# A hand-planned trunk kernel: the rank of weight preparation, and two constants of a matmul's estimate, in the planner that fixes the order of issue

## The chip, the cores and the metric

One Trainium2 chip, one of its cores. The metric is device time in microseconds (us) from launch to end; lower is better. TensorE (PE) multiplies, VectorE (DVE), ScalarE (ACT) and GpSimd (POOL) do elementwise work, and SyncE (SP) issues the loads.

## The reference

Two decoder layers on 256 tokens of width 1024, then a final RMSNorm, all in float32.

```
for layer in range(2):
    h = rms_norm(x, mix_norm[layer])
    x = x + (gdn_shortconv_mixer if layer == 0 else nsa_mixer)(h, ...)
    x = x + square(relu(rms_norm(x, mlp_norm[layer]) @ w_up)) @ w_down
return rms_norm(x, final_norm)

gdn_shortconv_mixer(h):                       # the first mixer
    qkv, z, a, b, b_gate, c_gate, hs = split(h @ w_in)
    q, k, v = silu(causal_conv4(qkv))         # 8 heads x 64
    g = -exp(a_log) * softplus(a + dt_bias);  beta = sigmoid(b)
    o = gated_delta_rule_chunked(l2norm(q), l2norm(k), v, g, beta)
    y_a = rms_norm(o) * silu(z);  y_b = b_gate * causal_conv3(c_gate * hs)
    return concat(y_a, y_b) @ w_out
```

The delta rule inverts a unit lower-triangular matrix for each head and each of two halves of the sequence (c = 0 and 1 here), and passes a state from the first half to the second. The second mixer is sparse attention with three branches.

## The kernel before

**Arithmetic.** A float32 weight is split in two fp32r halves: `uh` (ScalarE copies it to fp32r) and `ul` (VectorE subtracts `uh` from the weight in its staging tile `st`). Activations `x` are split likewise, and each product is three matmuls of 128x128 by 256 columns: `hi*xh`, `hi*xl`, `lo*xh` (`mm256`).

**Weights.** 105 MB stream through four staging tiles `st` (two units of 128x1024 each). A unit of weights is prepared by `splits(0)` or `splits(1)` (odd and even units): one ScalarE and one VectorE instruction. There are four buffers for prepared units (UB = 4); a unit's buffer is free again, and the next split may begin, when TensorE has read the unit (flag `ud`). An emptied staging tile lets SP issue its next load.

**Streams and planner.** All engines issue strictly in the order that the program was written in, and that order comes from `Order`, which plays the kernel through with estimated durations when it is built. The work is a set of generators, "streams". Each asks for an engine, a PSUM bank, a flag or a token. `run` picks the stream that could start earliest by the estimates; of several with the same start it picks the lower rank `prio`, then the older stream (index `i`). An engine with a queue of ready streams gives all of them the same start, so there the rank decides. The streams are: the loads (rank 0), the two `splits` (rank `SPLIT`), `main` (rank `MAIN` = 9, or -1 when its clock account `debt` is over a limit), which issues all projections and the matmuls of the MLPs in order, and whatever these spawn. A spawned stream without a rank of its own gets one here:

```
    def spawn(self, gen, prio=None):
        c = self.cur
        if prio is None:
            prio = 1 if c is None or c.prio in (MAIN, SPLIT) else c.prio
```

and an engine counts as free a little before its instruction ends (`OVER`: 80 ns on VectorE), while the next instruction of the same stream can start only at that end.

**The first mixer.** `main` issues the projections K (`proj_ko`, 8 units of 512 columns), z/a/b (`proj_tok`, 8 units of 528, twelve matmuls of 264 columns each), V, Q, C, H, B (`proj_m`, four units of 24 matmuls each) and the output projection (`proj_out`, 8 units; its units 0 to 3 read `yb` of the short convolution, 4 to 7 read `ya` of the delta rule). Beside it runs the chain (rank `CHAIN` = 0): the convolution of K (`conv_evac`: `pre`, a multiplication and three multiply-adds on `cvconv`, a tanh, a product into `K`; two `pre` buffers), `zab`, `betas`, `decay`, the norms of K (`chain_k`), and `chain_main` (solutions, state). Spawned from these, without a rank of their own: `spans` and its `products` (the decay masks `E`; `gt` on POOL or VectorE), `chain_q`, `invert(c)` (`keys`: `wide` on ScalarE, transposes on TensorE, `KB` on VectorE; `scores`: `al`; then `lc`, `tt`, `uc`, and for five levels matmuls of 32x32 with `ys`, `tt`, `uc` between), `diagonal` and `output` (`o`, `osq`, `oss`, `ya`). The convolutions of V, the evacuations of Q, C, H, B (`prepool`, `CG`, `bgt`), and `values` (`bv`) are spawned by `main`. Convolutions of Q and H run on POOL (`cvpool`, `CG`, `tap`). `Norm.finish` (the sum over squares, `ncol`, `rbc`) has rank 0 in all five norms.

**Estimates.** `Timed.cost` gives the planner a duration for each instruction; for a matmul it goes by the columns m of the weights and n of the moving operand. These estimates don't change what an instruction does.

Of the kernel before, what the change touches and what calls it, by code (L numbers as in the profile page):

```python
# [11 lines left out]
F32R = mybir.dt.float32r  # L12
# [20 lines left out]
PK, PW, PR, F1, GZ, ZP, LD, RT, P2 = 1, 0, 1, 1, 1, 1, 1, 21, 8  # L33
KPOOL, VPOOL, CVB = (), (), {'conv': 4, 'pool': 2}
CHAIN, TOK_FIRST = 0, False
TICK, BUSY = 10240 / 3, 1500.0
MAIN, SPLIT, SHARE, LIMIT, FLOOR, CAP, SPARE = 9, 0, 0.5, 300, -1500.0, 4000.0, 1
ORDER1 = ('kk', 'q0', 'kc', 'vg', 'cmp', 'q1', 'wo')


# [116 lines left out]
class Order:  # L157
# [44 lines left out]
    def spend(self, eng, cost, cols=0.0, port=False):  # L202

        c = self.cur
        start = max(self.free[eng], c.hold + self.IN[eng], c.t + self._lag(c, eng))
        if eng == 'PE':
            tick = int(start / TICK)
            if self.cols.get(tick - 1, 0.0) < BUSY:
                cost *= 2
            self.cols[tick] = self.cols.get(tick, 0.0) + cols  # L210
            gap = min(start - self.free[eng], 3000.0)
            self.debt = min(max(FLOOR, self.debt + SHARE * 2.4 * (cost + gap) - cols), CAP)
        elif eng == 'G':
            start = max(start, self.port[2])
            self.port[:2] = start, start + cost
        elif port:
            if self.port[0] - cost < start < self.port[1]:
                start = self.port[1]
            self.port[2] = start + cost
        c.t = start + cost  # L220
        self.free[eng] = c.t - self.OVER[eng]
        c.last = eng
# [27 lines left out]
    def run(self):  # L250
        while self.streams:
            best = None
            for i, s in enumerate(self.streams):
                t, at = self._start(s)
                prio = -1 if s.prio == MAIN and self.debt > self.limit else s.prio
                if t is not None and (best is None or (t, prio, i) < best[0]):
                    best = (t, prio, i), s, at
            assert best, [s.want for s in self.streams]
            _, s, at = best
            w, value = s.want, None  # L260
            if isinstance(w, (str, dict)):
                value = at
            else:
                s.hold = max(s.hold, at)
                if w[0] == 'bank':
                    slot = min(self.banks)
                    self.banks.remove(slot)
                    value = self.get_bank(slot[1])
                    self.held[id(value)] = slot[1], value
                elif w[0] == 'take':  # L270
                    self.tokens[w[1]].remove(min(self.tokens[w[1]]))
            self._next(s, value)
# [11 lines left out]
class Timed:  # L284
# [14 lines left out]
    def cost(self, op, a, k):  # L299
        aps = [x for x in list(a) + list(k.values()) if isinstance(x, bass.AP)]  # L300
        size = lambda x: int(np.prod(x.shape[1:]))
        if self.name != 'PE':
            return self.other(op, a, k, aps, size)
        rows = aps[1].shape[0]
        if op == 'transpose':
            return 0.85 * rows, rows * rows / 128
        m, n = size(aps[1]), size(aps[2])
        if aps[2].dtype == F32:
            if m <= 64 and aps[0].start_partition():
                return 8 + 0.7 * m, 0.0  # L310
            return max(1.75 * m, 1.68 * n), 4 * n * rows / 128
        return max((0.86 if aps[2].dtype == F32R else 0.25) * m, 0.46 * n), n * rows / 128

    def other(self, op, a, k, aps, size):
        n = max(size(x) for x in aps)
# [1545 lines left out]
```

## Time and profile before

| | us |
|---|---|
| median of 3 runs | 698.89 (697.01 to 701.65) |
| the profiled execution | 699.36 |
| its span, first to last instruction | 697.6 |
| TensorE busy in it | 664.7 (95%) |
| VectorE, ScalarE, POOL busy | 479.5, 388.1, 136.2 |

In the profiled execution the first mixer reaches from about 17 to 196 us, the first MLP to about 365, the second mixer to about 515, the second MLP and the final norm to the end. All instructions have line 294 (the helper that records them), so they are told apart by tile names; `b` is a PSUM bank.

### The profile page before, as it was taken

Reading aid. Unit: us, or ns where it says so; the run is one execution under the profiler, and the core shown is the slowest. Engines: PE = TensorE matmul, PEld = TensorE weight load, DVE = VectorE, ACT = ScalarE, POOL = GpSimd, SP = SyncE. Lnnn points to the kernel's source line nnn. Section 1 sums busy time; section 2 is a strip of 40 time slices with the busy share of each in tenths; the row PEclk is TensorE's granted clock in tenths of the full one; section 3 lists DMA queues with packets and bytes.
Section 4 is the critical chain, followed back from the end, with each engine's and each line's share of the span. In section 5 each row is a group of like instructions: output and inputs, shape, how many; then the busy total and the mean of one; then the engine's idle time right before and its main releaser. Section 6 shows DMA issues by size and latency. Waiting matters only on the chain.

```text
span 697.6 us, 15854 instructions
## 1 busy us (share of the span) xinstructions
PE 664.7 (95%) x6573; PEld 625.0 (90%) x6573; DVE 479.5 (69%) x898; ACT 388.1 (56%) x750; POOL 136.2 (20%) x177
## 2 busy tenths in 40 slices
PE   8998879996999999999999999999899999999994
PEld 6997779996999999999999876978699999999994
DVE  6999868674775556566568999997396655555452
ACT  7556223331588787444446567676478878544430
POOL 2035678100210000011013251212130000011121
PEclk9999989997999999999999999999999999999997
DMA  8843331311355555555553367213135555555501
GB/s 296 289 175 136 122 123 64 107 36 55 138 206 190 183 189 203 209 185 182 190 207 110 129 224 290 73 62 122 61 122 182 183 183 195 207 201 182 182 1 60
DMA packets 17640, 109.05 MB, mean 156 GB/s; under 512 B 2080, under 2 KB 2336, under 8 KB 5536
## 3 DMA queue, kind: packets, MB, share of 16 engines
q1 hardware_dynamic: 17280, 107.52, 44.1%
q8 instruction: 51, 0.84, 0.5%
q10 hardware_dynamic: 288, 0.52, 0.2%
q14 instruction: 21, 0.17, 0.1%
HBM read 106.99 MB, written 1.05 MB: 155 GB/s over the span
## 4 chain that ended last, share of the span: by engine, by line
PE 75%; DVE 16%; issue 3%; ACT 3%; DMA 1%; SPq 0%; POOL 0%; DVEq 0%; ACTq 0%; POOLq 0%
PE b L294 75%; DVE ul L294 4%; DVE cvconv L294 1%; DVE x L294 1%; ACT uh L294 1%; DVE kc L294 1%; DMA X<-xt 1%; DVE swq L294 1%; DVE rqt L294 1%; DVE X L294 1%; DVE nm L294 0%; ACT px L294 0%; DVE lc L294 0%; DVE qr L294 0%; DVE cm L294 0%
## 5 line engine op out<-in xcount | busy, mean ns | idle before, releaser
L294 DVE TENSOR_TENSOR ul<-st,uh 128x1024 fp32r<-128x1024 f32 (+3 forms) x204 | 244.2, 1200 | 143.4 <-ACT uh L294 141.1
L294 ACT ACTIVATE uh<-st 128x1024 fp32r<-128x1024 f32 (+3 forms) x204 | 205.8, 1011 | 195.3 <-PE b L294 179.6
L294 PE MATMUL b<-x,uh 128*128 128x256 f32 (+1 forms) x1632 | 295.5, 283 | 2.0 <-DVE x L294 0.8
L294 PEld LDWEIGHTS b<-x,uh 128*128 128x128 f32 x1632 | 249.4, 189 | 6.6 <-ACT uh L294 1.8
L294 PE MATMUL b<-x,ul 128*128 128x256 f32 x832 | 231.1, 279 | 0.7 <-DVE ul L294 0.6
L294 PE MATMUL b<-U,uh 128*128 128x256 f32 x1024 | 174.2, 276 | 0.0
L294 PEld LDWEIGHTS b<-x,ul 128*128 128x128 f32 x832 | 157.1, 189 | 1.8 <-DVE ul L294 1.5
L294 PEld LDWEIGHTS b<-U,uh 128*128 128x128 f32 x1024 | 154.1, 188 | 0.0
L294 PE MATMUL b<-U,ul 128*128 128x256 f32 x512 | 141.3, 276 | 0.0
L294 PEld LDWEIGHTS b<-U,ul 128*128 128x128 f32 x512 | 96.1, 188 | 0.0
L294 POOL TENSOR_TENSOR nacc<-nacc,sq 128x256 f32<-128x256 f32 x24 | 27.1, 1127 | 244.2 <-ACT sq L294 244.1
L294 ACT ACTIVATE px<-b,nm 128x128 f32<-128x128 f32 (+1 forms) x64 | 26.3, 423 | 10.0 <-DVE nm L294 9.7
L294 ACT ACTIVATE U<-u 128x256 fp32r<-128x256 f32 x64 | 26.8, 419 | 2.0
L294 ACT ACTIVATE u<-t 128x256 f32<-128x256 f32 x64 | 26.7, 418 | 2.0
L294 POOL TENSOR_TENSOR px<-px,den 128x128 f32<-128x128 f32 x32 | 17.3, 568 | 53.5 <-DVE den L294 39.1
L294 DVE TENSOR_TENSOR U<-u,U 128x256 fp32r<-128x256 f32 x64 | 27.0, 425 | 0.7 <-ACT U L294 0.7
L294 PE MATMUL b<-uh,x 128*128 128x264 f32 (+1 forms) x128 | 24.9, 290 | 0.0
L294 POOL TENSOR_TENSOR X<-X,par 128x256 f32<-128x256 f32 x8 | 5.5, 694 | 99.2 <-ACT nacc L294 90.2
L294 PE MATMUL b<-ohl,uh 128*128 128x256 f32 x128 | 24.6, 291 | 0.2
L294 ACT ACTIVATE t<-b 128x256 f32<-128x256 f32 x64 | 23.3, 364 | 0.0
L294 DVE SCALAR_TENSOR_TENSOR x<-X,par,x 128x256 fp32r<-128x256 f32 x32 | 19.1, 616 | 4.2 <-ACT x L294 4.1
L294 PEld LDWEIGHTS b<-ohl,uh 128*128 128x128 f32 x128 | 19.6, 189 | 0.9 <-ACT ohl L294 0.3
(274 smaller groups left out, 806.0 us busy)
## 6 DMA issues: line engine op xcount, KB each, us to landing
st<-wts SPq DMA_DIRECT2D x94, 1024.0 KB, 4.8
st<-wts SPq DMA_DIRECT2D x4, 560.0 KB, 3.7
st<-wts SPq DMA_DIRECT2D x4, 528.0 KB, 4.8
st<-wts SPq DMA_DIRECT2D x8, 256.0 KB, 5.4
X<-xt SPq DMA_DIRECT2D x3, 256.0 KB, 5.4
par<-par SPq DMA_DIRECT2D x1, 525.0 KB, 5.8
out_dram<-X SPq DMA_DIRECT2D x2, 256.0 KB, 2.6
out_dram<-X ACTq DMA_DIRECT2D x2, 256.0 KB, 3.1
```

The lines of the kernel that those rows point to most:

```text
L294: r = f(*a, **k)
```

## The change

`SPLIT` goes from 0 to 0.5. So the two `splits` rank behind streams of rank 0 and still ahead of those of rank 1. By the lines of `spawn` above a second thing follows: before, rank 0 was equal to `SPLIT`, so what the chain spawned got rank 1; now it inherits 0. `YIELD` adds a delay by rank to the start that `run` compares, but its three values are zero. The matmul's estimate for fp32r goes from max(0.86 m, 0.46 n) to max(0.885 m, 0.443 n) for n up to 256 and max(0.885 m, 0.455 n) beyond: for m = 128, n = 256 from 117.8 to 113.4 ns. No instruction is added or removed.

```
-MAIN, SPLIT, SHARE, LIMIT, FLOOR, CAP, SPARE = 9, 0, 0.5, 300, -1500.0, 4000.0, 1
+YIELD = (0.0, 0.0, 0.0)
+MAIN, SPLIT, SHARE, LIMIT, FLOOR, CAP, SPARE = 9, 0.5, 0.5, 300, -1500.0, 4000.0, 1
...
-                if t is not None and (best is None or (t, prio, i) < best[0]):
-                    best = (t, prio, i), s, at
+                if t is not None:
+                    key = t + (0.0 if isinstance(s.want, tuple) else YIELD[min(int(prio), 2)]), prio, i
+                    if best is None or key < best[0]:
+                        best = key, s, at
...
-        return max((0.86 if aps[2].dtype == F32R else 0.25) * m, 0.46 * n), n * rows / 128
+        return max((0.885 if aps[2].dtype == F32R else 0.25) * m, (0.443 if n <= 256 else 0.455) * n), n * rows / 128
```

## Rows read from the trace of the kernel before

**Rows 1.** Busy time by stretches: length, busy us (instructions) by engine, granted clock, DMA.

```profile
20.00:45.00 25.00, 24.72 (x208) 24.32 (x206) 24.41 (x68) 15.54 (x29) 0.00 (x0) 1.00 0.79 287
45.00:60.00 15.00, 13.37 (x102) 12.11 (x102) 14.47 (x23) 6.61 (x10) 10.39 (x8) 1.00 0.31 98
60.00:82.00 22.00, 20.42 (x168) 19.21 (x166) 20.28 (x44) 9.95 (x17) 15.97 (x17) 1.00 0.41 152
82.00:102.00 20.00, 14.17 (x441) 13.03 (x441) 13.70 (x30) 3.60 (x5) 10.83 (x14) 0.83 0.24 68
102.00:164.00 62.00, 62.00 (x1260) 57.31 (x1258) 44.33 (x103) 19.10 (x30) 20.68 (x25) 1.00 0.24 83
164.00:171.20 7.20, 1.79 (x7) 1.00 (x6) 4.08 (x13) 2.01 (x3) 1.26 (x1) 0.65 0.00 0
```

**Rows 2.** The same view of two later stretches: the first MLP, and the second mixer's end.

```profile
220.00:240.00 20.00, 20.00 (x179) 20.00 (x178) 11.62 (x15) 16.10 (x31) 0.00 (x0) 1.00 0.52 176
...
480.00:500.00 20.00, 17.84 (x141) 14.05 (x141) 11.57 (x23) 12.19 (x35) 5.20 (x8) 1.00 0.18 57
```

**Rows 3.** The timeline of TensorE where units 4 to 7 of the output projection begin.

```profile
168.70 1.08 PE L294 MATMUL b<-par,o 128*128 128x128 f32 x4 [4.58 <-DVE o L294]
170.47 1.31 PE L294 MATMUL b<-ya,uh 128*128 128x256 f32 x2 [0.69 <-ACT ya L294]
...
176.28 0.45 PE L294 MATMUL b<-ya,uh 128*128 128x256 f32 x2
...
178.07 0.39 PE L294 MATMUL b<-ya,uh 128*128 128x256 f32 x2
...
178.41 0.39 PE L294 MATMUL b<-ya,uh 128*128 128x256 f32 x2
```

**Rows 4.** The timeline of TensorE from 57 to 96 us: waits, and two triples.

```profile
57.25 1.06 PE L294 MATMUL b<-par,wide 128*128 128x128 f32 x8 [1.53 <-DVE preconv L294]
...
83.43 0.75 PE L294 MATMUL b<-tt,al 32*32 32x32 f32 x64 [1.42 <-DVE tt L294]
...
88.42 0.72 PE L294 MATMUL b<-ys,uc 32*32 32x32 f32 x62 [1.95 <-DVE ys L294]
...
95.05 0.43 PE L294 MATMUL b<-tt,al 32*32 32x32 f32 x14 [2.46 <-issue]
...
96.21 0.63 PE L294 MATMUL b<-x,uh 128*128 128x256 f32 x2
...
96.85 0.63 PE L294 MATMUL b<-x,uh 128*128 128x256 f32 x2
```

**Rows 5.** The timeline of VectorE, from the first convolution of K to the inversion.

```profile
19.70 1.95 DVE L294 TENSOR_TENSOR ul<-st,uh 128x528 fp32r<-128x528 f32 x3
21.58 0.42 DVE L294 TENSOR_TENSOR preconv<-b,rbc 128x256 f32<-128x256 f32 x1
...
37.65 1.21 DVE L294 TENSOR_TENSOR ul<-st,uh 128x1024 fp32r<-128x1024 f32 x1
38.79 0.41 DVE L294 SCALAR_TENSOR_TENSOR K<-K,cvconv 128x256 f32<-128x256 f32 x1
...
45.08 2.06 DVE L294 TENSOR_TENSOR ul<-st,uh 128x1024 fp32r<-128x1024 f32 x1
...
71.27 1.27 DVE L294 TENSOR_TENSOR KB<-K,b 128x512 f32<-128x512 f32 x2
...
86.84 1.18 DVE L294 TENSOR_TENSOR ul<-st,uh 128x1024 fp32r<-128x1024 f32 x1
87.95 0.41 DVE L294 TENSOR_TENSOR ys<-b,par 128x256 f32<-128x256 f32 x1
```

**Rows 6.** The timeline of TensorE at the first two triples of a z/a/b unit.

```profile
20.70 0.41 PE L294 MATMUL b<-uh,x 128*128 128x264 f32 x2
...
21.06 0.41 PE L294 MATMUL b<-uh,x 128*128 128x264 f32 x2
```

**Rows 7.** The timeline of POOL at 45 us.

```profile
45.02 5.21 POOL L294 TENSOR_TENSOR gt<-par,gp 128x512 fp32r<-128x512 f32 x4 [27.01 <-DVE gp L294]
```

## The prediction

> **What bounds the kernel now.** I read the busy time by stretches first. In the first MLP TensorE works 20.00 of 20.00 us with 179 matmuls [rows 2], one every 111.7 ns; no order of issue makes that shorter, and two MLPs of 3072 matmuls in all are 343 of the 698 us. In the second mixer there is little idle: the worst stretch has 2.2 of 20 us [rows 2]. The first mixer has most. Its stretches [rows 1] show three regimes. From 20 to 82 us VectorE is the full engine (24.41 of 25, 14.47 of 15, 20.28 of 22), and TensorE loses 0.3, 1.6 and 1.6 us. From 82 to 102 us neither is full and TensorE loses 5.8 us at a granted clock of 0.83 of 2.4 GHz. From 102 to 164 us TensorE is full, 62.00 of 62 us. From 164 to 171.2 us it loses 5.4 us, clock 0.65. That makes 14.7 us of idle in all, and the clock on top.
>
> Then the timeline at those places says who ends the waits. At the end TensorE has used up the short-convolution half of the output projection and stands 4.58 us for `o`, then 0.69 us for `ya`, the last steps of the chain [rows 3]; it then runs at the lower of its two levels (1.2 GHz) until 176.28. At 83.43 and 88.42 it stands for `tt` and `ys`, steps of the inversion; at 57.25 for `preconv`, an evacuation of V that had not freed its bank; at 95.05 for nothing that the profile shows ("issue") [rows 4].
>
> So the chain ends too late, and the question is where it was held. VectorE's timeline shows it [rows 5]: the transposes behind `KB` ran on TensorE at 57.25 [rows 4], and `KB` on VectorE at 71.27, 13 us after they ended, on an engine that was nearly full, behind splits and the convolutions of V. By the code that is no accident: `invert` was spawned by a stream whose rank equalled `SPLIT`, so it got rank 1, like V's convolutions, and lost every tie to older ones. The change's larger part is this: it lifts `invert`, `spans`, `products`, `chain_q`, `diagonal` and `output` from 1 to 0.
>
> **Part 1: the chain ahead (gain).** The convolution of K took from 21.58 to 39.13 us [rows 5]. Ten `ul` lay in between, five short (1.95 us for three, 0.65 each) and five long (from 37.65 to 38.79, 1.14 each), 8.9 us; so K could end up to 8.9 us earlier. `KB` could run right behind its transposes, 13 us earlier than it did. Not both in full: z/a/b's projection gates `beta`, `g` and the masks. I take the chain as 10 us earlier or more at `KB`. What the end needs is less: 4.58 + 0.69 us. The waits at the end then vanish, and their clock with them: from 170.47 to 176.28 there are eight triples of matmuls in 5.81 us; at the pace after it (178.07 to 178.41, 0.34 us a triple) they take 2.72. That is 3.1 us. Sum at the end: **8.4 us** (bounds 0, if the chain's lead is lost again in the full stretch, and 8.4). In the inversion `ys` at 87.95 stood behind an `ul` that began at 86.84; ranked ahead, it and `tt` would not: 1.42 + 1.95 = **3.4 us** (bounds 0 and 3.4). The 62 us that are full stay as long as they are; matmuls of the chain only change places with projections. What is late next is the POOL path of the short convolution and TensorE itself.
>
> **Part 2: the weights behind (loss).** A split that waits makes its unit late, with the unit its projection, and with the emptied staging tile SP's next load (DMA share 0.79 at 20 to 45 us, 0.31 after [rows 1], so a load that starts some us later still finds room; I cost that at nothing, as long as the unit itself is the later of the two). The cover is the lead: units made before TensorE needs them. At 21.58 three of the z/a/b units were just made [rows 5], and one lasts four triples of 0.36 us [rows 6], 1.45 us, so TensorE has work to about 24.6. If K's streams, two of which alternate on VectorE without a gap, shut the splits out for all of their 8.9 us, the next unit comes at about 31 and TensorE stands 6.4 us, then runs as much at 1.2 GHz as it did behind the wait at the end, 3.1 us: 9.5 us. At the other end the lag of ScalarE's tanh and the two `pre` buffers let splits through, and nothing is lost, as in the trace of before (24.72 of 25 us busy). Nothing excludes either; no row shows a K chain without splits between. I take the middle, **4.7 us**. Behind the waiting splits on VectorE stand also V's evacuations, at rank 1, and they hold banks: the one such stall is 1.53 us [rows 4]. The chain's steps now pass them; I take no more than that stall again, but charge it at zero because V's units are late too (bounds -1.5 and +3).
>
> One rule speaks against moving splits later. POOL's first block, four `gt` in 5.21 us from 45.02 [rows 7], falls on an `ul` of 2.06 us at 45.08, where another took 1.21 [rows 5]: 0.85 us more. The Trainium skill, SBUF — State Buffer, section "Who interferes with whom", says that a VectorE instruction with two SBUF inputs contends with a GpSimd one that reads SBUF and that the later of the two waits; by that rule, the trace agrees. POOL is idle from 20 to 45 us and busy 10.4 of the next 15 [rows 1]. If all eight long `ul` that fit in 8.9 us moved there, VectorE would lose 8 x 0.85 = 6.8 us in its full stretch; this is the price of the second rival.
>
> **Part 3: the rest.** `Norm.finish` now passes the splits in all norms; its eight small steps hide behind projections that read `x` without the norm, so nothing (bounds -0.5 and +0.5). The estimate of a matmul falls from 117.8 to 113.4 ns, with 111.7 measured; only the order changes by it. In the MLPs TensorE is full in any order: nothing. In the second mixer it can shift steps by some ns per matmul between two engines; its worst stretch idles 2.2 of 20 us [rows 2], so I take 0, with -2 and +2.
>
> **Sum.** Gain 8.4 + 3.4, loss 4.7: 7.1 us off the profiled execution's 699.36 (its span is 697.6, 1.8 us lie around it), 692.3. That execution stands 0.5 above the median of 698.89, so **692**. Its own range: 687 (loss at zero, less one for the mixer) to 697 (loss whole).
>
> **Rivals.**
> First, slower: the splits are shut out for good. The point from which it decides: the chain keeps VectorE for longer than the three units' 4.4 us, and does so again when `al` (two halves, 8 each) and `lc`, `tt` pass the evacuations of V. Then TensorE loses the 9.5 us, and a second time about as much when V's banks stay full, and gains 8.4 at the end: 699.4 + 19 - 8.4 - 3.4 = 706.6, some 704 to 710. For it: VectorE is full exactly there. Against: a single chain stream leaves a slot after each of its steps.
> Second, eaten: the chain's lead is paid for in full, by the starved units or by the 6.8 us of the shared port, 7.1 less 6.8, at 698.6 (695 to 702).
> Third, bigger: nothing is lost at the start (4.7 more) and, with other groups of small matmuls meeting the loads, the 2.46 us of "issue" at 95.05 goes, with its clock (a triple there takes 0.64 us, 96.21 to 96.85, against 0.34): 683 to 687, at 685. The Trainium skill, Runtime: NRT & Kernel Launch, section "Instruction fetch mechanics", says that fetching code is mostly hidden; if that holds here the wait at 95.05 is no fetch, and it can go with the order. That the wait stands inside one group of 64 matmuls, after the fiftieth, speaks against it, so I leave it in the forecast.
> Fourth, the change does nothing: ranks decide ties alone, and if the estimates made few of them the order stays: 698.9. `KB` behind V's convolutions speaks against it.
>
> **How the numbers follow.** A measurement of this kernel tells about 1% (7 us) from no change: the three runs span 4.6 us. Chances: forecast 0.48, second rival 0.23, slower 0.16, bigger 0.10, nothing 0.03. Of the forecast's range (687 to 697) just over half lies under 691.9: 0.26, with the bigger one 0.36; I round to 0.38. Slower by over 1% is the first rival and a tail of the second: 0.17. Within 1%: 0.45. The range from 684 to 704 leaves out most of the first rival and the end of the bigger one.
>
> **What would show it.** `KB` soon after its transposes, `K` done by 31 to 35 us instead of 39; no wait for `o` or `ya` before the output projection, and 2.4 GHz through it; waits for `ul` on TensorE between 24 and 32 us, the size of the loss. The forecast is wrong if those waits exceed the 8.4 us that the end gives, or if the waits at the end only move to a `bgt` or a POOL convolution.

## The result, and the profile after

The changed kernel takes 703.71 us (median of 10 runs, 701.12 to 712.01) against 697.90 for the kernel before (10 runs beside it). The ratio is 1.0072, 95% interval 1.0046 to 1.0098: some 5 us slower, where 692 was forecast. One of the ten executions, that of 712.01, was in a slow state, and ratios here and below are of fast executions alone. The profiled execution took 703.5 us, its span 701.7 us; the one of before had 697.6, so 4.1 us are to be found. (The helper line is 297 in the changed kernel.)

First the same stretches as in [rows 1, 2], and 400 to 420 us, for which the row of before stands last; columns as there.

```profile
20.00:45.00 25.00, 19.51 (x140) 19.14 (x138) 19.52 (x53) 11.02 (x19) 0.00 (x0) 0.86 0.59 207
45.00:60.00 15.00, 14.83 (x119) 13.86 (x118) 14.41 (x36) 7.81 (x16) 5.33 (x4) 1.00 0.25 90
60.00:82.00 22.00, 17.61 (x370) 16.08 (x368) 19.94 (x49) 8.42 (x10) 2.19 (x2) 0.95 0.48 160
82.00:102.00 20.00, 15.67 (x395) 14.82 (x396) 12.80 (x34) 4.21 (x7) 15.86 (x22) 0.84 0.30 105
102.00:164.00 62.00, 61.46 (x1077) 57.11 (x1077) 41.38 (x99) 20.55 (x33) 27.05 (x33) 0.99 0.25 84
164.00:171.20 7.20, 7.20 (x63) 7.20 (x62) 5.55 (x14) 2.92 (x4) 1.82 (x1) 1.00 0.07 27
...
400.00:420.00 20.00, 15.10 (x94) 12.79 (x94) 18.84 (x44) 11.92 (x45) 8.15 (x17) 0.91 0.38 142
...
480.00:500.00 20.00, 20.00 (x161) 17.15 (x159) 13.39 (x30) 14.27 (x44) 1.55 (x4) 1.00 0.29 106
```
```profile
400.00:420.00 20.00, 19.07 (x132) 14.36 (x132) 19.28 (x49) 12.76 (x45) 10.46 (x20) 1.00 0.58 205
```

Length less TensorE's busy time, stretch by stretch, is what it idles. Before [rows 1]: 0.28 + 1.63 + 1.58 + 5.83 + 0 + 5.41 = 14.73 us. After: 5.49 + 0.17 + 4.39 + 4.33 + 0.54 + 0 = 14.92 us. The idle time of the first mixer has moved from its end to its beginning and is as long as it was. Its low clock moved too: 0.65 at the end became 1.00, and 1.00 at the beginning became 0.86.

The timeline of TensorE after, which answers to [rows 3, 4], shows where it now stands (start, length, what runs, in brackets the wait before it and who ended it):

```profile
23.70 0.41 PE L297 MATMUL b<-uh,x 128*128 128x264 f32 x2
29.60 0.59 PE L297 MATMUL b<-ul,x 128*128 128x264 f32 x1 [5.49 <-DVE ul L297]
...
30.64 0.64 PE L297 MATMUL b<-uh,x 128*128 128x264 f32 x2
...
31.30 0.64 PE L297 MATMUL b<-uh,x 128*128 128x264 f32 x2
...
36.58 0.40 PE L297 MATMUL b<-uh,x 128*128 128x264 f32 x2
...
36.95 0.28 PE L297 MATMUL b<-uh,x 128*128 128x264 f32 x1
...
53.84 1.03 PE L297 MATMUL b<-par,wide 128*128 128x128 f32 x8
...
78.53 1.54 PE L297 MATMUL b<-tt,al 32*32 32x32 f32 x128 [2.42 <-DVE tt L297]
82.06 0.77 PE L297 MATMUL b<-x,uh 128*128 128x256 f32 x2 [2.00 <-DVE ys L297]
...
100.37 0.78 PE L297 MATMUL b<-x,uh 128*128 128x256 f32 x2 [3.66 <-issue]
...
175.03 0.39 PE L297 MATMUL b<-ya,uh 128*128 128x256 f32 x1 [0.42 <-DVE ya L297]
...
401.64 0.37 PE L297 MATMUL b<-uh,x 128*128 128x280 f32 x1 [2.63 <-DVE t L297]
...
403.93 0.40 PE L297 MATMUL b<-uh,x 128*128 128x280 f32 x1 [1.66 <-ACT px L297]
```

The wait for `o` is gone. In its place there is one wait of 5.49 us for a split (`ul`) in the projection of z/a/b, ending at 29.60, and behind it a triple of matmuls takes 0.66 us (30.64 to 31.30) until 35.65, against 0.37 from 36.58 to 36.95. The inversion's waits, `tt` and `ys`, and the one put down to "issue" are all still there: 2.42, 2.00 and 3.66 us, where before they were 1.42, 1.95 and 2.46. At 400 us, in the second mixer, stand two waits that before had no like: that stretch had 19.07 of 20 us busy then, and 15.10 now.

VectorE's timeline after answers to [rows 5]:

```profile
20.15 1.33 DVE L297 TENSOR_TENSOR ul<-st,uh 128x528 fp32r<-128x528 f32 x2
...
28.84 0.70 DVE L297 TENSOR_TENSOR ul<-st,uh 128x528 fp32r<-128x528 f32 x1
...
30.81 0.42 DVE L297 SCALAR_TENSOR_TENSOR K<-K,cvconv 128x256 f32<-128x256 f32 x1
...
55.80 1.27 DVE L297 TENSOR_TENSOR KB<-K,b 128x512 f32<-128x512 f32 x2
...
75.77 1.78 DVE L297 STREAM_TRANSPOSE lc<-al 32x256 f32<-32x256 f32 x4
77.58 0.43 DVE L297 TENSOR_TENSOR tt<-lc,par 128x256 f32<-128x256 f32 x1
78.05 0.43 DVE L297 TENSOR_TENSOR tt<-tt,par 128x256 f32<-128x256 f32 x1
...
79.66 1.18 DVE L297 TENSOR_TENSOR ul<-st,uh 128x1024 fp32r<-128x1024 f32 x1
80.76 0.47 DVE L297 SCALAR_TENSOR_TENSOR cvconv<-preconv,par,cvconv 128x256 f32<-128x256 f32 x1
81.17 0.42 DVE L297 TENSOR_TENSOR preconv<-b,rbc 128x256 f32<-128x256 f32 x1
...
81.50 0.41 DVE L297 TENSOR_TENSOR ys<-b,par 128x256 f32<-128x256 f32 x1
```

Between the `ul` that end at 21.48 and the one at 28.84 VectorE runs the convolution of K and no split.

So each sign that the prediction named came true: `K` is done at 31.2 us instead of 39.2, `KB` runs at 55.80, right behind its transposes at 53.84, and not at 71.27; the output projection starts without a long wait and at 2.4 GHz; a wait for `ul` stands between 24 and 32 us. Yet the last matmul of the output projection begins at 185.7 us, 1.4 us later than before. These groups by tile show it, for the two kernels (count, then shortest/median/longest ns, then when the first and the last began). Before:

```profile
L294 DVE SCALAR_TENSOR_TENSOR E<-b,rk,E x16: 308/341/351, 122.9 to 149.8; 128x128 f32<-128x128 f32 x16
...
L294 ACT ACTIVATE Q<-cvpool x4: 399/417/417, 77.3 to 100.2; 128x256 f32<-128x256 f32 x4
...
L294 PE MATMUL b<-ya,uh x64: 276/276/580, 170.5 to 184.3; 128*128 128x256 f32 x64
```

After:

```profile
L297 DVE SCALAR_TENSOR_TENSOR E<-b,rk,E x16: 338/345/351, 130.5 to 158.2; 128x128 f32<-128x128 f32 x16
...
L297 ACT ACTIVATE Q<-cvpool x4: 398/417/420, 96.0 to 114.5; 128x256 f32<-128x256 f32 x4
...
L297 PE MATMUL b<-ya,uh x64: 276/276/393, 174.2 to 185.7; 128*128 128x256 f32 x64
```

The chain led by 15 us at `KB` and trails by 8 us at the attention scores `E`. Q's last part is made at 114.5 us, 100.2 before; that it is late because its evacuations, spawned by `main`, have rank 1 is likely and not shown. The lead never reaches the end: the last product into `o` before `ya` begins at 170.4 us, 167.9 before. The end is rid of its wait because the projections before it are later too. From there to the last matmul of the second mixer's output projection it is 328.0 us, 325.3 before: 2.7 us more, beside the 1.4. Both make the 4.1. The marks are starts of the last matmuls with `uh`.

### The profile page after: what moved, and what is told of

It is laid out like the page before. It is cut to its first block, busy times and chain, and to the rows that moved or that the text cites. A ratio compares the mean times of both kernels' runs of the same rounds, so it can differ in the third digit from the quotient of the medians.

```text
span 701.7 us, 15831 instructions
## 1 busy us (share of the span) xinstructions
PE 665.0 (95%) x6573; PEld 628.9 (90%) x6573; DVE 469.3 (67%) x889; ACT 393.0 (56%) x762; POOL 130.8 (19%) x174
## 4 chain that ended last, share of the span: by engine, by line
PE 80%; DVE 13%; ACT 3%; issue 2%; DMA 1%; SPq 0%; DVEq 0%; ACTq 0%
PE b L297 80%; DVE ul L297 4%; ACT uh L297 1%; DVE cvconv L297 1%; DVE x L297 1%; DMA X<-xt 1%; DMA st<-wts 1%; DVE rqt L297 1%; DVE X L297 1%; DVE kc L297 1%; DVE nm L297 0%; DVE KL L297 0%; DVE qr L297 0%; SPq L429 0%; DVE swq L297 0%
## 5 line engine op out<-in xcount | busy, mean ns | idle before, releaser
L297 DVE TENSOR_TENSOR ul<-st,uh 128x1024 fp32r<-128x1024 f32 (+3 forms) x204 | 241.5, 1187 | 154.4 <-ACT uh L297 152.2
L297 PE MATMUL b<-uh,x 128*128 128x264 f32 (+1 forms) x128 | 30.2, 321 | 4.3 <-DVE t L297 2.6
L297 ACT ACTIVATE px<-b,nm 128x256 f32<-128x256 f32 (+1 forms) x64 | 26.5, 434 | 9.3 <-DVE nm L297 9.3
L297 PEld LDWEIGHTS b<-uh,x 128*128 128x128 f32 x128 | 23.8, 216 | 4.8 <-issue 2.8
L297 PE MATMUL b<-ul,x 128*128 128x264 f32 (+1 forms) x64 | 20.5, 320 | 5.5 <-DVE ul L297 5.5
L297 POOL TENSOR_TENSOR px<-px,den 128x128 f32<-128x128 f32 x32 | 14.8, 489 | 49.0 <-DVE den L297 30.9
```

The lines of the kernel that those rows point to most:

```text
L297: r = f(*a, **k)
```

## The experiments

The change bundles three things: the splits go behind rank 0 (`SPLIT`), the chain's children rise from 1 to 0 (by `spawn`), and the estimate of a matmul falls. The theory after the traces: the first two cancel in the first mixer, what the one gains at the end the other loses at the start, and the estimate adds a loss of its own. The rivals: the estimate does nothing and the splits' rank is the whole loss; or the children's rise is worth nothing. e1 to e5 take the parts one by one and in pairs; every edit is made to the kernel before. Three marks are taken from each profile: the end of the first mixer (start of the last matmul of `ya` and `uh`), from there to the first `VT`, a step inside the second mixer, and to the last matmul on `ohl`, the end of the second mixer's output projection (the first MLP lies in between). The marks are of one execution each. Those of e1 (704.75 us) and e7 (701.01) were 6.0 and 4.8 us over their kernel's median, so their first marks are not typical.

| kernel | median us (runs) | ratio, 95% interval | first mixer ends | to `VT` | to mixer 2's end |
|---|---|---|---|---|---|
| before | 697.90 (10) | 1 | 184.3 | 227.0 | 325.3 |
| after | 703.71 (10) | 1.0072 (1.0046 to 1.0098) | 185.7 | 238.1 | 328.0 |
| e1, ranks of the change, estimate of before | 698.77 (12) | 1.0018 (0.9992 to 1.0045) | 189.8 | 227.0 | 325.4 |
| e8, the same kernel, one execution | 698.43 (1) | | 182.1 | 227.0 | 326.6 |
| e2, estimate alone | 716.94 (6) | 1.0259 (1.0234 to 1.0285) | 198.0 | 237.9 | 327.8 |
| e3, children up alone | 691.39 (6) | 0.9900 (0.9877 to 0.9923) | 176.7 | 227.1 | 325.4 |
| e4, splits back alone | 709.16 (6) | 1.0147 (1.0116 to 1.0177) | 191.9 | 226.9 | 324.9 |
| e5, children up and estimate | 705.32 (6) | 1.0095 (1.0068 to 1.0122) | 186.7 | 239.4 | 329.2 |
| e6, estimate 0.45 n | 721.41 (5) | 1.0317 (1.0284 to 1.0349) | 197.4 | 235.6 | 335.0 |
| e7, splits back after z/a/b | 696.20 (12) | 0.9974 (0.9942 to 1.0006) | 185.2 | 226.9 | 326.1 |
| e9, estimate 0.475 n | 719.56 (6) | 1.0294 (1.0267 to 1.0321) | 205.1 | 232.6 | 327.2 |
| e10, e3 with 0.475 n | 699.01 (12) | 1.0006 (0.9988 to 1.0023) | 181.7 | 232.6 | 327.2 |
| e11, e5, account at old cost | 710.02 (5) | 1.0169 (1.0145 to 1.0194) | 186.2 | 237.4 | 333.7 |
| e12, estimate 0.461 n | 716.39 (6) | 1.0243 (1.0214 to 1.0271) | 195.9 | 226.8 | 331.7 |

**e1: both ranks, the old estimate.**

```
-MAIN, SPLIT, SHARE, ... = 9, 0, 0.5, ...
+MAIN, SPLIT, SHARE, ... = 9, 0.5, 0.5, ...
```

> SPLIT 0.5 as in the change, the matmul's estimate as before. Theory S (the starved weights in K's convolution and the late Q path pay for the chain's lead in the first mixer; the second mixer's loss of 2.7 us comes with the new estimate's order): first mixer ends 1 to 2 us later than before, second mixer as before, 0.0 to +2.5 us in all. Rival L (the order of issue is a lottery: any change of a rank or an estimate moves each mixer by some us either way): the second mixer moves by 2 us or more here too, with no pattern.

Measured 1.0018: the two ranks together change nothing that can be told from the noise. TensorE has the wait for `ul` (5.5 us) and none for `o`, as in the changed kernel, and 7.8 us of "issue" in three places.

**e2: the estimate alone.**

```
-        return max((0.86 if aps[2].dtype == F32R else 0.25) * m, 0.46 * n), ...
+        return max((0.885 if aps[2].dtype == F32R else 0.25) * m, (0.443 if n <= 256 else 0.455) * n), ...
```

> The matmul's estimate as in the change, SPLIT 0. Theory S: no wait for ul of 5 us near 25 us, the first mixer within 1.5 us of before, the second mixer 2 to 3 us longer, in all +1 to +4 us. Rival L: either sign, either mixer, up to 4 us.

Measured 1.0259, 18 us slower: the edit that the prediction put at nothing is the largest of the three when it is made alone, and neither theory (at most 4 us) had it. `KB` comes still later than before, and the end of the first mixer is empty (groups by tile, then busy time by stretches):

```profile
L294 DVE TENSOR_TENSOR KB<-K,b x2: 674/674/675, 76.3 to 76.9; 128x512 f32<-128x512 f32 x2
```
```profile
164.00:176.00 12.00, 10.08 (x92) 9.50 (x88) 1.55 (x4) 1.77 (x3) 0.00 (x0) 0.64 0.00 1
176.00:186.00 10.00, 2.62 (x9) 1.76 (x10) 6.38 (x16) 2.17 (x3) 1.26 (x1) 0.50 0.00 0
```

The chain is later, the projections are used up before it ends, and TensorE works 2.62 of 10 us at 1.2 GHz (waits: `o` 6.6 us, `ys` 3.9, `Vf` 3.5).

**e3: the children up alone.**

```
-            prio = 1 if c is None or c.prio in (MAIN, SPLIT) else c.prio
+            prio = 1 if c is None or c.prio == MAIN else c.prio
```

> Only the spawn rule changed: what the chain spawns has rank 0, the splits stay at rank 0 and, being older, win ties against all of it; the estimate as before. Theory S: no wait for ul of 5 us near 25 us, KB by 60 us as in the changed kernel, the end of the first mixer 3 to 8 us earlier than before: 690 to 696 us. If the chain's lead is lost in the Q path alone (rival Q), the first mixer ends within 1.5 us of before even without the starved weights.

Measured 0.9900, 7 us faster: the only version that beats both kernels by a margin. Its stretches, then two groups:

```profile
20.00:45.00 25.00, 24.81 (x209) 24.50 (x208) 24.52 (x68) 15.76 (x29) 0.00 (x0) 1.00 0.78 281
45.00:60.00 15.00, 13.61 (x105) 12.79 (x105) 13.56 (x25) 6.14 (x10) 9.95 (x6) 1.00 0.35 128
60.00:82.00 22.00, 16.55 (x338) 15.28 (x338) 20.38 (x58) 5.97 (x9) 2.83 (x2) 0.77 0.31 105
82.00:102.00 20.00, 18.10 (x556) 16.93 (x556) 13.96 (x29) 5.27 (x7) 18.98 (x24) 1.00 0.22 68
102.00:164.00 62.00, 61.05 (x969) 57.24 (x968) 46.43 (x106) 22.56 (x36) 25.09 (x32) 1.00 0.23 84
164.00:171.20 7.20, 7.20 (x66) 7.20 (x65) 4.36 (x5) 2.63 (x4) 0.00 (x0) 1.00 0.66 215
```
```profile
L294 DVE TENSOR_TENSOR KB<-K,b x2: 674/682/689, 58.9 to 61.3; 128x512 f32<-128x512 f32 x2
...
L294 PE MATMUL b<-ya,uh x64: 276/276/284, 166.1 to 176.7; 128*128 128x256 f32 x64
```

`KB` comes 12 us earlier, no wait for `ul` appears (24.81 of 25 us busy), and the end is full at 2.4 GHz. Idle: 0.19 + 1.39 + 5.45 + 1.90 + 0.95 + 0 = 9.88 us, 4.85 less than before. The stretches from 45 to 102 us keep theirs, 8.74 us against 9.04: `tt` 3.2, `ys` 2.4, `al` 1.4, `gt` 1.3. Here the chain's lead does reach the end: the last product into `o` begins at 162.4 us, 5.5 earlier than before.

**e4: the splits behind rank 0, the children left at 1.**

```
-MAIN, SPLIT, SHARE, ... = 9, 0, 0.5, ...
+MAIN, SPLIT, SHARE, ... = 9, 0.5, 0.5, ...
...
-            prio = 1 if c is None or c.prio in (MAIN, SPLIT) else c.prio
+            prio = 1 if c is None or c.prio in (MAIN, 0) else c.prio
```

> SPLIT 0.5, but what the chain spawns keeps rank 1; the estimate as before. Theory S: the 5 us wait for ul near 25 us with the lower clock behind it, K early, KB as late as before relative to it, so nothing is gained in return: 4 to 9 us slower than before, 702 to 707 us. Rival Q: the starved weights cost only what the end gives back, within 2 us of before.

Measured 1.0147, 10.3 us slower, more than either theory had. Its waits (engine and tile that wait, who ended it: us in all, times, longest) hold the start's and the end's side by side:

```profile
PE b L294 <- DVE ul L294: 5.5, 1, 5.5
PE b L294 <- DVE o L294: 4.9, 1, 4.9
```

So at the old estimate -7.0 and +10.3 add to +3.3, and together they measured +1.3: additive within the noise (some 2 us on each), and nearly nothing.

**e5: the children up, with the changed estimate** (the edits of e3 and e2).

> The chain's children at rank 0, the splits at rank 0 as before, and the matmul's estimate of the change. Theory S, extended (the new estimate costs the second mixer 2.5 us in whatever company, and the first mixer only where the chain's children rank low): first mixer within 2 us of the run with the children up alone (its last ya matmul at 176.7 us), second mixer 2.5 us longer: 693 to 697 us. Rival L (each plan is a draw): the first mixer ends 4 us or more away from 176.7 us, or the second mixer keeps its 325.4 us.

Measured 1.0095. Beside e2 the children's rise is worth 11.6 us here by the medians; beside e3 the estimate costs 13.9. The first mixer ends 10.0 us later than e3's, as rival L had it. Against e5 the changed kernel, which also puts the splits back, is no slower (1.0072): at this estimate that edit costs nothing, at the old one (e1 beside e3) 7.4 us by the medians. The parts do not add across estimates.

**e6: the estimate halfway, old ranks.**

```
-        return max((0.86 if aps[2].dtype == F32R else 0.25) * m, 0.46 * n), ...
+        return max((0.86 if aps[2].dtype == F32R else 0.25) * m, 0.45 * n), ...
```

> All ranks as before, the fp32r matmul estimated at 0.45 ns per column: 115.2 ns for 256 columns, between 117.8 and 113.4. If a cheaper matmul in the plan harms by degrees, the first mixer ends 4 to 10 us later than before and the whole is at 703 to 712 us. Rival L: it lies anywhere from 692 to 717 us, beyond both ends included, and the second mixer takes either 325.4 or 328 us with no step between.

Measured 1.0317, worse than the whole step (e2): the time is not monotone in the estimate. It is not halfway in every part: beyond 256 columns 0.45 lies under e2's 0.455.

**e7: the splits behind rank 0 only after the first 16 units** (K's and z/a/b's), to take away the wait for `ul`. `SPLIT` is 0.5, and `splits` sets its own rank, unit by unit (i):

```
+            order.cur.prio = 0 if i < 16 else SPLIT
```

> SPLIT 0.5 and the chain's children at 0, but the sixteen units of the projections K and z/a/b are split at rank 0; the estimate as before. Theory S: the 5.5 us wait for ul near 25 us and its lower clock go, the rest stays: 4 to 9 us faster than with the splits behind throughout, 690 to 695 us, equal to or better than the children up alone. If the starved weights are not the price, it stays within 2 us of 698.8.

Measured 0.9974, 2.6 us better than e1 by the medians; the two intervals overlap. The wait for `ul` shrinks from 5.5 to 0.8 us, but the inversion's grow (`ys` 4.7, `tt` 3.5), and it doesn't reach e3 (4.8 us slower). So the early units seem to be a part of what e4 lost, and not all of it: past z/a/b it still pays to leave the splits at rank 0.

**e8: e1 once more, a single execution**, since e1's profiled execution was long (704.75 against a median of 698.77).

> The same kernel as with SPLIT 0.5 and the old estimate, one more profile, because that run's profiled execution was 6 us over its median and showed three waits without a cause (issue) of 7.8 us together. If these are what varies from execution to execution, a typical one has under 4 us of them and its first mixer ends 4 to 6 us earlier than 189.8 us; if it is the order itself, they stand at the same three places again.

The "issue" waits did not vary: 7.2 us in four places, 7.8 in three in e1. What differed is the granted clock. First e1, then e8:

```profile
122.00:142.00 20.00, 20.00 (x246) 18.34 (x245) 11.35 (x31) 5.00 (x8) 10.19 (x13) 0.72 0.15 54
```
```profile
122.00:142.00 20.00, 20.00 (x315) 18.32 (x315) 13.33 (x36) 5.41 (x10) 14.28 (x17) 1.00 0.32 106
```

**e9 and e10: the estimate dearer**, 0.475 n, at the old ranks and with the children up (the line of e6 with 0.475; e10 with that of e3 too). The theory under test was that a cheaper matmul lets projections pass the chain, so that a dearer one should do the reverse.

> All ranks as before, the fp32r matmul at 0.475 ns per column instead of 0.46: 121.6 ns for 256. Theory M (a cheaper matmul in the plan lets the projections and their evacuations, at rank 1 and older, pass the chain: KB from 71.3 to 76.3 us in both cheaper runs, the first mixer 13 us later): the other way round here, KB before 71 us, the chain's last ya before 170 us, the first mixer 2 to 8 us shorter, 690 to 697 us. Rival W (0.46 is the lucky draw of many, and any other value loses): slower than 702 us, as both cheaper values were.

> The chain's children at rank 0, the splits at 0, and 0.475 ns per column. Theory M: the chain is ahead by rank already, so a dearer matmul adds little: within 4 us of the children up alone (691.4), either side. Rival W: slower than 697 us.

Measured 1.0294 and 1.0006. That theory falls: 0.475 is as bad as 0.45, and `KB` comes at 76.5 us with it, 76.3 with both cheaper ones. e10 is 7.6 us slower than e3, outside the 4 us of theory M. The children's rise is worth 20.5 us here.

**e11: e5 with the clock account at the old cost.** `main`'s rank depends on `debt`, which sums estimated costs; this kernel corrects the matmuls of 256 columns in that sum alone.

```
-            self.debt = min(max(FLOOR, self.debt + SHARE * 2.4 * (cost + gap) - cols), CAP)
+            self.debt = min(max(FLOOR, self.debt + SHARE * 2.4 * (cost * (0.46 / 0.443 if cols == 256 else 1) + gap) - cols), CAP)
```

> Children up with the change's estimate (705.3 us), but the planner's clock account, which gives main rank -1 when few columns were sent, still goes by the old estimate of 256 columns. If the account is how the estimate harms the first mixer, that mixer ends near the 176.7 us of the children up alone and the whole is at 693 to 698 us; the second mixer keeps its 3 us, since the account is off there. If it is the planned time of the matmuls themselves, 702 us or more.

Measured 1.0169, slower than e5, with the first mixer's end where e5 has it (186.2 and 186.7 us): putting the account right does not give the loss back.

**e12: the estimate by a hair**, 0.461 n at the old ranks: 0.26 ns more on 117.8.

> All ranks as before, the fp32r matmul at 0.461 ns per column instead of 0.46: 118.0 against 117.8 ns for 256, a fifth of a per cent. Rival W (0.46 is one good plan among many, and any other value is another plan): 5 us or more away from the kernel before, and slower. Theory B (there is a basin around 0.46 and the planner needs the estimate right to a few per cent): within 3 us of it.

Measured 1.0243, 17 us slower, with `KB` at 73.6 us. The first mixer ends 11.6 us later. `VT` follows it as before, and TensorE loses 6.4 us more later in the second mixer (17.05 of 20 us busy from 420 to 440 us).

## Why the prediction was wrong, step by step

**Part 1, the end: right for e3, by luck in the changed kernel.** The 8.4 us for the wait and its clock are there in e3: 5.41 us of idle at the end gone and 3.1 of clock, less the 0.95 us newly lost in the full stretch, make 7.6; the first mixer ends 7.6 us earlier (184.3 to 176.7), and the time falls by 7.0 (the ratio). This sum takes the end alone: from 60 to 102 us e3's clock costs more than before (0.77 of 2.4 GHz in 16.55 busy us, some 3.8 us) and gives some 2.4 back (1.00 for 0.83 in 14.17), so by all stretches the sum is about 6.6. In the changed kernel the chain did not end earlier, as the `o` at 170.4 us shows: the bound of 0, the lead lost in the full stretch, held for the chain. There the wait went because the projections before it came later (the last matmul on `yb` at 173.8 us, 163.7 before).

**Part 1, the inversion: wrong, a step of it.** "Ranked ahead, it and `tt` would not" stand behind an `ul`: 3.4 us were booked, and the idle time from 45 to 102 us stayed at 9.04 (before), 8.89 (after) and 8.74 (e3). VectorE's rows of before could have told it for `tt`:

```profile
80.68 1.78 DVE L294 STREAM_TRANSPOSE lc<-al 32x256 f32<-32x256 f32 x4
...
82.95 0.43 DVE L294 TENSOR_TENSOR tt<-tt,par 128x256 f32<-128x256 f32 x1
```

No split stands among these, and of the 1.95 us for `ys` at 88.42 the `ul` at 86.84 [rows 5] fills 1.18 at most. VectorE's rows of after show the same. From 75.77 to 78.48 it runs the four `lc` and two `tt` back to back, 2.64 us with no split among them, and TensorE's wait of 2.42 us ends with the last: this is the chain's own length, which no rank shortens. And `ys` at 81.50 stands again after an `ul` that began at 79.66, while TensorE still worked for it (until 80.07), and after two steps of V's convolution of rank 1 (80.76 and 81.17). A rank decides between equal planned starts alone; by the rule of `run`, steps of a higher number go ahead of `ys` only if its planned start was later than theirs.

**Part 2, the splits: the term was mis-sized.** The place, the time and the sort of wait were as worked out (5.49 us at 29.60; 6.4 at 31 were worked out). The middle of 0 and 9.5 was the wrong choice. Behind the wait 6.05 us (29.60 to 35.65) ran at 0.66 us a triple instead of 0.37, 2.7 us lost; with the wait 8.2 us, where 4.7 was taken. e4, the edit alone, costs 10.3 us. The reason given for the lower end, that tanh's lag and two `pre` buffers let splits through, did not hold: VectorE made no split from 21.48 to 28.84 us, and TensorE had no unit from about 24 to 29.6. In e7, with the early units at rank 0, that wait shrinks to 0.8 us.

So in the first mixer it was the second rival, "eaten": some 8.4 gained, 8.2 lost. It was eaten by the starved units and not by the shared port: of the 21 long `ul` from 45 to 164 us the median took 1.22 us (1.23 before) and the longest 2.06 (2.11). The mixer ended 1.4 us later; towards that go 0.54 us of idle in the full stretch, 0.42 for `ya` at 175.03 and some 0.9 by the clock of 0.95 in 60 to 82 us (17.61 x 0.05). This account by idle and clock closes within about one us for the changed kernel and for e3, but not for e8, which by the same sum should end later than before and ends 2.2 us earlier; "busy" matmuls have modelled ends, and a full stretch can hide a different pace.

**Part 3, the estimate: a step that failed.** "I take 0, with -2 and +2." Beside e1, the same ranks with the old estimate, the changed kernel is 1.0072 / 1.0018, 0.54% or 3.8 us slower, and at other ranks the same edit costs 13.9 (e5 beside e3) and 18 us (e2). The argument was that the first MLP is full in any order, and that the second mixer idles little. The first half holds. The second half takes the plan as given: the estimate doesn't shift steps by nanoseconds in one plan, it makes another plan. The column to `VT` shows that. Whatever the ranks, the six profiles with 0.46 (before, e1, e3, e4, e7, e8) have 226.9 to 227.1 there; those with 0.443 have 237.4 to 239.4, those with 0.475 232.6, that with 0.45 235.6 (0.461 has 226.8, and loses 6.4 us behind it). In the changed kernel the second mixer's largest loss is the stretch of 400 to 420 us with its two waits of 2.63 and 1.66 us, 3.97 us of idle more than before; 480 to 500 us gives 2.16 us back (20.00 busy, 17.84 before, [rows 2]), and 2.7 us remain at the second mixer's end. The six profiles with 0.46 have 324.9 to 326.6 there, the eight with another estimate 327.2 to 335.0. In which mixer the changed kernel's 3.8 us lie is not settled: beside before it loses 2.7 in the second, but beside e8, which has its ranks and ran as near to its median, 3.6 in the first and 1.4 in the second.

That 113.4 ns is nearer than 117.8 to the 111.7 that TensorE takes did not help: 0.461, 0.475, 0.45 and 0.443 all lost 17 to 22 us at the old ranks. What the runs show is that the kernel before sits on a good plan whose neighbours are 2 to 3% worse, most of it in the first mixer (11.6 to 20.8 us). `KB` is late in all four (73.6 to 76.5 us, 71.3 before), but that is not the whole cause: with the children up, where the times start from 691 and reach 699 and 705, `KB` is no later than e3's (57.8 and 57.3 us against 58.9), and the first mixer still ends 5.0 and 10.0 us later. That 0.46 is itself nothing but a lucky value is the likeliest reading, not shown: four neighbours are few. By which decision of the planner either mixer goes astray stays open; correcting the account alone (e11) did not help. Not tried is the planner's own clock rule: `spend` doubles a matmul's planned cost where it takes the clock to be low, and which matmuls that hits can change with any planned start.

**The chances.** "Eaten" had 0.23 and is what the ranks did; no case priced the estimate at more than 2 us. The time, 703.71, lies between the ranges of "eaten" (695 to 702) and "slower" (704 to 710), and the latter's mechanism, a second starving, did not come. By the ratios, edit by edit: the children up gave 7.0 us (e3) where 11.8 were forecast, the splits behind them cost 8.2 (e1 beside e3) where 4.7 were taken, the estimate cost 3.8 (the change beside e1) where 0 was taken; -7.0 + 8.2 + 3.8 is the 5.0 measured. The profiles give a like account, each of the three terms erring the same way: 5.6 us at the inversion's three named waits (3.4 expected off; with "issue" they grew by 2.3 instead), 3.5 at the splits, 2.7 in the second mixer make 11.8; the 1.53 us for `preconv` [rows 4], which is gone, brings it to 10.3, of the 11.2 between the 7.1 forecast and the 4.1 found in the profile, the other way. Two slips of the working change nothing: K's last step ends at 39.20 us, not 39.13, and the lower end of the range, by its own words, would be 686.

## What to carry to other kernels

A producer that ranks behind two alternating consumers of a full engine should, after this case, be costed as shut out for all that they take beyond its lead, with the low clock behind the wait, not at a middle. Before a wait is booked as a queue's, look whether the engine that ends it ran the chain's own steps back to back; then no rank removes it. And where a planner fixes the order, a constant of it is not a small edit, however much nearer to the measurement: make the parts of a bundle one by one, and several near values of the constant, before one is believed; here the part worth having (children up, 0.9900) lay hidden in a bundle that was slower.

## What was not expected of the hardware

The same program had a granted clock of 0.72 in one execution and 1.00 in another, in the same stretch from 122 to 142 us, with TensorE busy 20.00 of 20 us by the profile in both; the first mixer ended at 189.8 and 182.1 us. So one profile of this kernel can be 6 us off its median by a stretch that looks full.

Waits of TensorE that the profile puts down to nothing ("issue") are no noise: 7.8 and 7.2 us in two executions of one program, 2.46 us before, 3.66 after, 0.5 in e3. The traces say what they go with. The list of DMA queues has one that it calls `q8 instruction`, with 51 transfers of some 16 KB in an execution, and one of them falls into each of the two waits, of before (92.59 to 95.05 us) and of after (96.71 to 100.37). The queue's row (transfers, MB, share of 16 engines) from 92 to 93 us before, then from 97 to 98 us after:

```profile
q8 instruction: 1, 0.02, 6.0%
```
```profile
q8 instruction: 1, 0.02, 5.9%
```

All 17 such waits of 0.3 us or more that the fourteen profiles have between 20 and 200 us end 2.2 to 2.6 us after a transfer of this queue began, while the transfers come 3.6 to 8.2 us apart where before has its wait. So these waits go with fetching code (the loading of the program's next instructions), and they change with the order. The prediction weighed the Trainium skill, Runtime: NRT & Kernel Launch, section "Instruction fetch mechanics", by which fetching code is mostly hidden. The traces agree in the count: at most four of the 51 transfers of an execution come with such a wait; those that do cost up to 3.66 us. The third rival took from that rule that the wait at 95.05 is no fetch and so can go with the order. By these rows it goes with a fetch, and in e3, by another order, it went all the same.
